# When a late vector is accumulated, and where the softmax reciprocals stand

## The chip, the cores and the metric

The kernel runs on one core of a Trainium2 chip. The metric is device time in microseconds (us) of one execution of the whole program. Shorter is better.

## The reference

A trunk of two layers over a sequence of 1024 tokens of width 1024, all in float32. Layer 0 mixes tokens by forgetting attention with 16 heads, layer 1 by gated linear attention. Each mixer is followed by a SwiGLU channel mixer with 2816 hidden units. Shift, scale and gate of each sub-layer come from six vectors of length 1024 per layer, which are `silu(c)` times a slice of `ada_w`. Cut to what the change touches:

```python
c_act = jax.nn.silu(c)
for i in range(DEPTH):
    mod = c_act @ ada_w[i] + ada_b[i]
    sh1, sc1, g1, sh2, sc2, g2 = jnp.split(mod, N_MOD, axis=-1)
    h = modulate(rms_norm(x, norm1_g[i]), sh1, sc1)
    y = forgetting_attention(h, ...) if i % 2 == 0 else gated_linear_attention(h, ...)
    x = x + g1[:, None, :] * y
    h = modulate(rms_norm(x, norm2_g[i]), sh2, sc2)
    x = x + g2[:, None, :] * swiglu(h, ffn_w_in[i], ffn_w_out[i])

# forgetting attention, per block of 128 queries and head
logits = q @ k.T * scale + cum[q] - cum[k]      # causal
p = jax.nn.softmax(logits, axis=-1)
o = p @ v
```

## The kernel before

**Matrix products** are made of float32 operands split in a high and a low part. Helper `mm3` (L316) issues three matmuls for one product of blocks (L317, L318, L319). The low part of a split is a subtraction on VectorE (`split`, L174: cast on ScalarE at L175, subtraction on VectorE at L176).

**Attention** (L1326 to L1477) works in units (p, a, g): pair of heads p (0 to 7), head a of the pair, and group g of two query blocks of 128 rows. Groups run in the order 0, 3, 1, 2. For each of the two rows of a unit, `scores` (L1327) issues the score matmuls into a ring of two PSUM banks (L1348, L1350, and a mask matmul at L1352), in pieces of up to 512 keys. VectorE adds the forget term to each piece, writes it to the SBUF tile `lp` and takes the row minimum (L1356, a custom instruction and the read of its accumulator into `st`). ScalarE takes the exponential of the whole row and its sum (L1360), VectorE the reciprocal of the sum (L1361), and GpSimd multiplies the row by it (L1362). The next score matmul but one needs the bank that L1356 frees. One unit later, `outputs` (L1365) transposes the finished rows on TensorE (L1382), splits them (L175, L176), multiplies them by the values (L1396, L1394) and adds up the result (L1411, L1412). `weave` (L130) interleaves attention with projections for the next pair of heads (`qk_proj`, whose results go through L894 to L911, and `v_half`), as work that fills TensorE.

**The channel mixer** (`ffn`, L1579) computes its first product in 22 groups (11 blocks of hidden units, gate and up). The first two groups are plain tiles, the other 20 are seven products each of half-size blocks (`prod`, L1733; evacuated by `add`, L1745, and L1905). The weights of each product are loaded to `xv_s`, combined on GpSimd (L978 to L990) and split (L175, L176). The second product runs in three chunks of four groups, of 3, 4 and 4 blocks. The first two chunks are the loop at L1930 (L1956 adds PSUM onto SBUF on VectorE; in the second chunk GpSimd combines blocks at L1970 to L1974 and VectorE applies the gate at L1977). In the second chunk, group by group, GpSimd combines weights (L978 to L980, L996) and then the group's results (L1970 to L1974), while VectorE evacuates, splits weights and applies the gate (L1977) to what GpSimd combined, adding `x` as read back from HBM (loads at L1889). Blocks of hidden units for the third chunk are loaded on SP by `fetch` (L1860); the first block of the third chunk's second tile name, `T1o020`, takes the space of `z2`, which GpSimd reads last at L1973 of the third group, and what follows it in SP's order is issued behind it. The third chunk is at L2024.

**The vectors of layer 1 that are computed beside layer 0's channel mixer:** vectors 5 of layer 0 and 0 of layer 1 go through the queue `ada1` (L543). Vector 1 of layer 1, the scale of its first norm, goes through the queue `ada1l`: `ada_one` (L487) has 16 steps, each a load of 256 KB into `far` (four DMAs at L454 on the SP queue) and two instructions of VectorE that accumulate onto `near` (L497 once, then L499). Each `prod` pays `late_rate[0] * n` into this queue (L1740; n is the depth of the product, 4 in the groups, 3 or 4 in the chunks), and a step is issued when enough has been paid: a load costs 1.5, its two accumulations 0.5. The rate is 0.03 from the start, and 0.12 from the last group but one on (L1902). What is left is flushed behind the second chunk (L1989), and layer 1's first norm needs the vector behind the third.

**Order.** The order in which instructions stand on each engine comes from a list scheduler that works on the whole program. `issue_after`, `behind_one` (L257) and `behind_all` add constraints to it that carry no wait on the chip: an instruction then stands behind another one of the same engine. An engine executes in that order.

## Time and profile before

| | us |
|---|---|
| median of 3 runs | 2345.26 |
| lowest and highest of them | 2344.12, 2349.59 |
| the profiled execution | 2345.56 |
| span of the profiled execution, first to last instruction | 2343.8 |
| attention woven with projections | about 100 to 580 of the span |
| the 20 groups of layer 0's first channel product | about 700 to 1058 |
| first, second and third chunk of its second product | about 1058 to 1130, 1130 to 1205, 1205 to 1250 |

The profile lists for each engine its instructions with start, duration, and, where the engine was idle before one, for how long and which instruction released it. "Idle" and "busy" are of one engine; PE is TensorE, PEld its weight loads, DVE is VectorE, ACT ScalarE, POOL GpSimd, and SP the engine that issues DMAs. Matmuls overlap: 128 partitions by 512 columns take 0.39 us each, and start every 0.23 us. A matmul's end is modelled, so that TensorE reads as busy for a little into every wait.

### The profile page before, as it was taken

What the parts mean: (1) busy time and instruction counts of PE and PEld (TensorE: products, weight loads), DVE (VectorE), ACT (ScalarE), POOL (GpSimd) and SP (SyncE); (2) the same over time, 40 slices, a digit from 0 to 9 for tenths busy, and PEclk for the clock granted to TensorE, in tenths of its full rate; (3) what the DMA queues carried; (4) which work ended last, traced back from release to release, by engine and by line L of the source; (5) the groups of instructions that cost most, each with busy time, mean ns of one, the idle gap of its engine ahead of it and who ended that gap; (6) DMA issues with size and microseconds to landing.
All of it is one profiled execution on the core that took longest, in us unless ns stands there. A gap on an engine that the chain in (4) does not pass through costs nothing.

```text
span 2343.8 us, 35552 instructions
## 1 busy us (share of the span) xinstructions
PE 2322.6 (99%) x12088; PEld 1980.6 (85%) x12088; DVE 1772.7 (76%) x2946; ACT 1128.0 (48%) x2166; POOL 1160.5 (50%) x1027
## 2 busy tenths in 40 slices
PE   8999999999999999999999999999999999999999
PEld 7988888888888888788888899898888888888888
DVE  6577677776788888997888666668787777876787
ACT  6566566675544333334325654345444333345236
POOL 1345454533446656665563522345456666664651
PEclk9999999999999999999999999999999999999999
DMA  8533343352435545459774443555434544458674
GB/s 259 163 99 112 109 120 107 113 169 84 153 100 175 187 158 176 154 203 315 267 265 155 136 128 99 151 171 172 150 102 162 174 147 159 141 189 300 237 264 141
DMA packets 359342, 390.72 MB, mean 167 GB/s; under 512 B 26908, under 2 KB 296376, under 8 KB 359160
## 3 DMA queue, kind: packets, MB, share of 16 engines
q1 hardware_dynamic: 359160, 388.45, 50.7%
q8 instruction: 95, 1.56, 0.3%
q14 instruction: 87, 0.71, 0.1%
HBM read 287.10 MB, written 101.25 MB: 166 GB/s over the span
## 4 chain that ended last, share of the span: by engine, by line
PE 54%; DVE 4%; DMA 3%; POOL 2%; issue 2%; SPq 0%; ACT 0%; POOLq 0%; DVEq 0%; ACTq 0%
PE p_b L317 11%; PE p_b L319 11%; PE p_b L318 11%; PE gv_b L317 1%; PE gv_b L319 1%; PE gv_b L318 1%; PE gr_b L317 1%; PE gr_b L319 1%; PE gr_b L318 1%; DVE o_s L176 1%; DVE ad_s L543 1%; DMA ex_s<-x_sp 1%; PE gqp_b L317 0%; PE gk_b L317 0%; PE f1a_b L319 0%
## 5 line engine op out<-in xcount | busy, mean ns | idle before, releaser
L175 ACT CAST o_s<-xv_s 128x512 fp32r<-128x512 f32 (+1 forms) x392 | 235.9, 610 | 328.4 <-PE p_b L319 218.5
L176 DVE TENSOR_TENSOR o_s<-xv_s,o_s 128x512 fp32r<-128x512 f32 (+1 forms) x392 | 332.7, 854 | 37.2 <-ACT o_s L175 36.3
L317 PE MATMUL p_b<-B,o_s 128*128 128x512 f32 x608 | 235.4, 391 | 0.9 <-DVE ex_s L1745 0.5
L318 PE MATMUL p_b<-B,o_s 128*128 128x512 f32 x608 | 236.1, 389 | 0.0
L319 PE MATMUL p_b<-B,o_s 128*128 128x512 f32 x608 | 235.1, 389 | 0.0
L978 POOL TENSOR_TENSOR ex_s<-xv_s,xv_s 128x512 f32<-128x512 f32 (+1 forms) x64 | 96.0, 1499 | 238.8 <-DMA xv_s<-in_ffn_w_in_dram 123.3
L1362 POOL TENSOR_SCALAR lp_s<-lp_s,st 128x128 f32<-128x128 f32 (+7 forms) x128 | 98.9, 775 | 220.9 <-DVE st L1361 191.8
L317 PE MATMUL p_b<-T,o_s 128*128 128x512 f32 x480 | 186.7, 390 | 1.8 <-DVE x L1745 1.8
L318 PE MATMUL p_b<-T,o_s 128*128 128x512 f32 x480 | 186.7, 389 | 0.0
L319 PE MATMUL p_b<-T,o_s 128*128 128x512 f32 x480 | 181.2, 389 | 0.0
L1360 ACT ACTIVATE lp_s<-lp_s,st 128x128 f32<-128x128 f32 (+7 forms) x128 | 99.5, 777 | 85.4 <-DVE st L1356 68.1
L317 PEld LDWEIGHTS p_b<-B,o_s 128*128 128x128 f32 x608 | 114.1, 188 | 26.6 <-issue 1.6
L319 PEld LDWEIGHTS p_b<-B,o_s 128*128 128x128 f32 x608 | 114.1, 188 | 23.9
L318 PEld LDWEIGHTS p_b<-B,o_s 128*128 128x128 f32 x608 | 114.2, 188 | 23.2
L980 POOL TENSOR_TENSOR xv_s<-ex_s,xv_s 128x512 f32<-128x512 f32 (+1 forms) x64 | 95.7, 1495 | 51.2 <-DVE o_s L176 47.9
L1745 DVE TENSOR_TENSOR ex_s<-ex_s,p_b 128x512 f32<-128x512 f32 x140 | 94.2, 680 | 29.9 <-PE p_b L319 29.6
L990 POOL TENSOR_TENSOR xv_s<-xv_s,xv_s 128x512 f32<-128x512 f32 x48 | 65.8, 1370 | 97.9 <-issue 54.7
L176 DVE TENSOR_TENSOR pt_s<-t_b,pt_s 128x512 fp32r<-128x512 f32 (+1 forms) x160 | 98.4, 632 | 20.3 <-ACT pt_s L175 19.1
L317 PEld LDWEIGHTS p_b<-T,o_s 128*128 128x128 f32 x480 | 90.1, 188 | 21.3 <-DVE x L1745 2.2
L175 ACT CAST pt_s<-t_b 128x512 fp32r<-128x512 f32 (+1 forms) x160 | 82.6, 544 | 51.1 <-PE t_b L1382 32.6
L319 PEld LDWEIGHTS p_b<-T,o_s 128*128 128x128 f32 x480 | 90.1, 188 | 18.7
L318 PEld LDWEIGHTS p_b<-T,o_s 128*128 128x128 f32 x480 | 90.1, 188 | 18.6
(1539 smaller groups left out, 7378.2 us busy)
## 6 DMA issues: line engine op xcount, KB each, us to landing
xv_s<-in_ffn_w_in_dram SPq DMA_DIRECT2D x176, 256.0 KB, 3.2
hid_B<-x SPq DMA_DIRECT2D x66, 512.0 KB, 3.0
ad_s<-in_ada_w_dram SPq DMA_DIRECT2D x384, 64.0 KB, 2.4
hid_T<-x SPq DMA_DIRECT2D x44, 512.0 KB, 2.9
xv_s<-in_ffn_w_out_dram SPq DMA_DIRECT2D x88, 256.0 KB, 3.6
T2o<-hid_T SPq DMA_DIRECT2D x22, 512.0 KB, 7.0
T1o<-hid_T SPq DMA_DIRECT2D x22, 512.0 KB, 6.2
B11o<-hid_B SPq DMA_DIRECT2D x22, 512.0 KB, 5.9
```

Of the source, the lines that this page charges most:

```text
L175: nc.scalar.copy(hi, src)
L176: nc.vector.tensor_sub(lo, src, hi.bitcast(F32))
L317: nc.tensor.matmul(ps, ah, bh, start=start, stop=False, skip_group_check=chain)
L318: nc.tensor.matmul(ps, ah, bl, start=False, stop=False, skip_group_check=chain)
L319: nc.tensor.matmul(ps, al, bh, start=False, stop=stop, skip_group_check=chain)
L543: nc.vector.scalar_tensor_tensor(acc, raw[:, t], c42[:, o:o + 1], acc, op0=ALU.mult, op1=ALU.add)
L978: nc.gpsimd.tensor_add(s1, a21, a22)
L980: nc.gpsimd.tensor_sub(a11, s1, a11)
L990: nc.gpsimd.tensor_sub(r[A12], r[A12], r[A11])
L1360: nc.scalar.activation(lp, lp, AF.Exp, bias=mcur, scale=-1.0, accum_out=st[:, qi, 2:3])
L1362: nc.gpsimd.tensor_scalar(lp, lp, st[:, qi, 3:4], 1.0, op0=ALU.mult, op1=ALU.mult)
L1745: nc.vector.tensor_add(d, d if src is None else dest(G, src), ps)
```

## The change

```diff
--- before.py
+++ after.py
@@ -568,7 +568,7 @@
             while self.q:
                 self(1.0)
 
-    late_rate = [0.03]
+    late_rate = [0.0]
     ada0, ada0p, ada1, ada1l = Pace(), Pace(), Pace(), Pace()
 
     def ada1_queue(js, acc, raws_):
@@ -1358,8 +1358,11 @@
                 mcur = mnew
                 yield max(0.22, 0.00085 * (k1 - k0))
             nc.scalar.activation(lp, lp, AF.Exp, bias=mcur, scale=-1.0, accum_out=st[:, qi, 2:3])
-            nc.vector.reciprocal(st[:, qi, 3:4], st[:, qi, 2:3])
-            nc.gpsimd.tensor_scalar(lp, lp, st[:, qi, 3:4], 1.0, op0=ALU.mult, op1=ALU.mult)
+        at = last_of("D")
+        for qi in range(2):
+            with behind_one("D", at):
+                nc.vector.reciprocal(st[:, qi, 3:4], st[:, qi, 2:3])
+            nc.gpsimd.tensor_scalar(lps[qi], lps[qi], st[:, qi, 3:4], 1.0, op0=ALU.mult, op1=ALU.mult)
         return lps
 
     def outputs(u, lps):
@@ -1899,7 +1902,7 @@
             up = lambda n: advance(n) if X is gs[-1] else None
             if X is gs[-2]:
                 ada1.flush()
-                late_rate[0] = 0.12
+                late_rate[0] = 0.17
                 nxt[0] = part(0)
                 advance(4)
             nc.scalar.copy(dest(X, C11), prod(feed.next(), B11))
```

It has two parts. In `scores` the reciprocal and the multiplication of a row leave the row's loop: they come behind both rows, and each reciprocal is bound to stand behind the unit's last instruction on VectorE (the accumulator read of the last row's last piece). No instruction is added or removed, and no wait. And the late vector is paid for at 0.00 instead of 0.03 in the groups, and at 0.17 instead of 0.12 from the last group but one on. The first load is still issued at the first product, because the queue's account starts at zero.

The scheduler then orders all of attention and layer 0's channel mixer anew; before attention and from the third chunk on, the order of TensorE is the same. Three places are shown. Line numbers in rows of the changed kernel are 3 higher from L1362 on (L1364 is the reciprocal, L1385 the transposition, L1396/L1397 become L1399/L1400 and so on), and numbers at the end of names are those of buffers and tiles.

**VectorE at unit (2, 0, 3)**, the long unit at the start of the third pair of heads. `st203` is its statistics tile and `lp2030`, `lp2031` its two rows; `s206..`, `s207..` are its score pieces. Before:

```order
L1356 ISA lp2030_s45_29_2552,st203_2554<-s206512_b1_52_2562,cum4_s43_5_2034,st203_2554 128x384
L1356 ISA st203_2554 128x1
L176 TENSOR_TENSOR pt1120_s50_38_2500<-t1120_b3_38_2495,pt1120_s50_38_2500 128x512
L1361 RECIPROCAL st203_2554<-st203_2554 128x1
L1356 ISA lp2031_s46_30_2553,st203_2554<-s2070_b0_53_2578,cum4_s43_5_2034 128x512
L1356 ISA st203_2554 128x1
L247 TENSOR_TENSOR w1408_l_s24_24_2691<-w1408__s16_22_2688,w1408_h_s23_23_2690 128x256
L1356 ISA lp2031_s46_30_2553,st203_2554<-s207512_b1_54_2582,cum4_s43_5_2034,st203_2554 128x512
L1356 ISA st203_2554 128x1
L896 SCALAR_TENSOR_TENSOR QA3_2457<-qk031_b7_18_2571,QA3_2457 64x512
L898 SCALAR_TENSOR_TENSOR QB3_2458<-qk031_b7_18_2571,QB3_2458 64x512
L1356 ISA lp201_s47_31_2625,st201_2626<-s2020_b0_55_2627,cum4_s43_5_2034 128x384
```

With the change:

```order
L1356 ISA lp2031_s46_30_2553,st203_2554<-s2070_b0_53_2576,cum4_s43_5_2034 128x512
L1356 ISA st203_2554 128x1
L1356 ISA lp2031_s46_30_2553,st203_2554<-s207512_b1_54_2580,cum4_s43_5_2034,st203_2554 128x512
L1356 ISA st203_2554 128x1
L1364 RECIPROCAL st203_2554<-st203_2554 128x1
L247 TENSOR_TENSOR w1408_l_s24_24_2691<-w1408__s16_22_2688,w1408_h_s23_23_2690 128x256
L896 SCALAR_TENSOR_TENSOR QA3_2457<-qk031_b7_18_2571,QA3_2457 64x512
L898 SCALAR_TENSOR_TENSOR QB3_2458<-qk031_b7_18_2571,QB3_2458 64x512
L176 TENSOR_TENSOR pt2000_s50_41_2610<-t2000_b3_41_2606,pt2000_s50_41_2610 128x384
L1356 ISA lp201_s47_31_2625,st201_2626<-s2020_b0_55_2627,cum4_s43_5_2034 128x384
L1356 ISA st201_2626 128x1
L1364 RECIPROCAL st203_2554<-st203_2554 128x1
```

The first row's reciprocal stood ahead of the second row's first minimum, and now stands behind the second row's last; the second row's follows behind the next unit's first minimum (before, it stood some ten rows further down than shown).

**TensorE at the same place.** `s20..` are score pieces of the pair, `o11..` outputs of the unit before, `t20..` transposed rows, `vps`, `qk` projections that fill. Before, from the second piece of the second row on (its first piece, `s2070`, stands directly ahead):

```order
L1348 MATMUL s207512_b1_54_2582<-KA2_1686,QA2_1684 128x512
L1350 MATMUL s207512_b1_54_2582<-KLA_201,QA2_1684 128x512
L1382 MATMUL t2000_b3_41_2606<-ident_67,lp200_s48_28_2451 128x128 x3
L1348 MATMUL s2020_b0_55_2627<-KA2_1686,QA2_1684 128x384
L1350 MATMUL s2020_b0_55_2627<-KLA_201,QA2_1684 128x384
L1352 LDWEIGHTS identb_72
L1352 MATMUL s2020_b0_55_2627<-maskb_84,identb_72 128x128
L1348 MATMUL s2030_b1_56_2638<-KA2_1686,QA2_1684 128x512
L1350 MATMUL s2030_b1_56_2638<-KLA_201,QA2_1684 128x512
```

With the change, ahead of the next unit's first piece (ahead of the first row shown stand the two matmuls of `s207512` and nine of `o112`):

```order
L317 MATMUL vps20_b6_19_2708<-wv2560_0h_s19_19_2193,h0h2_179 128x256
L1399 MATMUL o112_b5_16_2494<-pt1122_s49_40_2521,v02_s29_3_924 128x256
L1397 MATMUL o112_b5_16_2494<-pt1122_s49_40_2521,v02_s29_3_924 128x128 x2
L318 MATMUL vps20_b6_19_2708<-wv2560_0l_s20_20_2194,h0h2_179 128x256
L319 MATMUL vps20_b6_19_2708<-wv2560_0h_s19_19_2193,h0l2_180 128x256
L317 MATMUL vps20_b6_19_2708<-wv2560_0h_s19_19_2193,h0h3_181 128x256
L318 MATMUL vps20_b6_19_2708<-wv2560_0l_s20_20_2194,h0h3_181 128x256
L1348 MATMUL s2020_b0_55_2627<-KA2_1686,QA2_1684 128x384
L1350 MATMUL s2020_b0_55_2627<-KLA_201,QA2_1684 128x384
```

Five score pieces (`s2070`, `s207512`, `s2020`, `s2030` and, behind the last row shown and its mask, `s2040`) followed each other with no projection between them. Now outputs and five projection matmuls stand between `s207512` and `s2020`.

**VectorE in the groups of layer 0's first product**, where the split weight `o008s` of its ninth block of hidden units is made. `p0_b..` are PSUM banks of products, `o00..`, `o01..` split weights. Before:

```order
L1745 TENSOR_TENSOR ex_s25_7229<-ex_s53_7228,p0_b1_94_9863 128x512
L543 SCALAR_TENSOR_TENSOR ad5_s47_7746<-ad5_s47_7746,c42_165 128x256
L176 TENSOR_TENSOR o008s_s24_108_9900<-ex_s53_7228,o008s_s24_108_9900 128x512
L499 SCALAR_TENSOR_TENSOR near_85<-far_86,c42_165,near_85 128x256 x2
L1745 TENSOR_TENSOR x0_0_6138<-x0_0_6138,p0_b6_91_9804 128x512
L1745 TENSOR_TENSOR ex_s53_7228<-ex_s53_7228,p0_b2_95_9880 128x512
```

With the change:

```order
L543 SCALAR_TENSOR_TENSOR ad5_s47_7746<-ad5_s47_7746,c42_165 128x256 x2
L1748 TENSOR_TENSOR x0_0_6138<-x0_0_6138,p0_b6_91_9774 128x512
L1748 TENSOR_TENSOR ex_s25_7229<-ex_s53_7228,p0_b1_94_9833 128x512
L176 TENSOR_TENSOR o01711_s48_105_9810<-xv_s17_7232,o01711_s48_105_9810 128x512
L176 TENSOR_TENSOR o008s_s24_108_9870<-ex_s53_7228,o008s_s24_108_9870 128x512
L1748 TENSOR_TENSOR ex_s53_7228<-ex_s53_7228,p0_b2_95_9850 128x512
```

The two accumulations of the late vector (L499) are gone from ahead of the evacuation of bank 6 (L1745, with the change L1748), and the evacuation stands ahead of a weight's split. 

**VectorE in the second chunk**, at the start of its second group (`z01`, `x0_2` and `x0_3` are that group's tiles). Before:

```order
L176 TENSOR_TENSOR o031ss_s45_190_11672<-ex_s53_7228,o031ss_s45_190_11672 128x512
L1956 TENSOR_TENSOR z01_10947<-z01_10947,p0_b7_37_11658 128x512
L176 TENSOR_TENSOR o03200_s23_191_11693<-xv_s18_7233,o03200_s23_191_11693 128x512
L1956 TENSOR_TENSOR x0_3_6141<-x0_3_6141,p0_b0_38_11675 128x512
L176 TENSOR_TENSOR o032s_s24_192_11716<-ex_s53_7228,o032s_s24_192_11716 128x512
L1956 TENSOR_TENSOR x0_2_6140<-x0_2_6140,p0_b1_39_11696 128x512
L1956 TENSOR_TENSOR x0_3_6141<-x0_3_6141,p0_b1_39_11696 128x512
L176 TENSOR_TENSOR o03200_s21_193_11735<-xv_s18_7233,o03200_s21_193_11735 128x512
L1956 TENSOR_TENSOR x0_2_6140<-x0_2_6140,p0_b2_40_11721 128x512
```

With the change:

```order
L176 TENSOR_TENSOR o031ss_s45_190_11666<-ex_s53_7228,o031ss_s45_190_11666 128x512
L499 SCALAR_TENSOR_TENSOR near_85<-far_86,c42_165,near_85 128x256
L1959 TENSOR_TENSOR z01_10911<-z01_10911,p0_b7_37_11650 128x512
L499 SCALAR_TENSOR_TENSOR near_85<-far_86,c42_165,near_85 128x256
L176 TENSOR_TENSOR o03200_s23_191_11691<-xv_s18_7233,o03200_s23_191_11691 128x512
L1959 TENSOR_TENSOR x0_3_6141<-x0_3_6141,p0_b0_38_11669 128x512
L176 TENSOR_TENSOR o032s_s24_192_11714<-ex_s53_7228,o032s_s24_192_11714 128x512
L1959 TENSOR_TENSOR x0_2_6140<-x0_2_6140,p0_b1_39_11694 128x512
L1959 TENSOR_TENSOR x0_3_6141<-x0_3_6141,p0_b1_39_11694 128x512
L176 TENSOR_TENSOR o03200_s21_193_11735<-xv_s18_7233,o03200_s21_193_11735 128x512
L499 SCALAR_TENSOR_TENSOR near_85<-far_86,c42_165,near_85 128x256 x2
L1959 TENSOR_TENSOR x0_2_6140<-x0_2_6140,p0_b2_40_11719 128x512
```

Each `L499` is one accumulation. A pair now stands around the second evacuation of `z01`, behind the split `o031ss`, which GpSimd's next combination waits for; the next pair stands behind the group's other evacuations. Seven pairs stand in the second chunk, where none stood: one in the first group ahead of its combinations on GpSimd; then in the second group the two shown and one between the split `o03201` and the gate of `x0_3`; and in the third group three more at the like places. On SP the four DMAs of each of their loads move there too, among the loads of weights (L960), of gate inputs (L1889, with the change L1892) and of blocks (L1860, with the change L1863).

## Prediction

> **What bounds the kernel now.** I read the page's busy times first, then the windows by stage, then the list of waits of TensorE.
>
> ```profile
> span 2343.8 us, 35552 instructions
> ...
> PE 2322.6 (99%) x12088; PEld 1980.6 (85%) x12088; DVE 1772.7 (76%) x2946; ACT 1128.0 (48%) x2166; POOL 1160.5 (50%) x1027
> ```
>
> TensorE is busy for 2322.6 of 2343.8 us, and the change leaves it its work. So all that can be won is in the 21.2 us in which it is idle, in what hides in modelled ends, and in a lowered clock; the rest is whether a new wait opens. The windows give, for each stretch, its length, the busy time of PE, PEld, DVE, ACT and POOL, the granted clock, the DMA share and GB/s:
>
> ```profile
> 232.00:236.00 4.00, 2.39 (x10) 1.14 (x10) 3.86 (x10) 3.27 (x7) 2.63 (x4) 0.97 0.54 155
> 236.00:240.00 4.00, 4.00 (x23) 4.00 (x23) 2.47 (x9) 1.19 (x3) 2.69 (x4) 0.61 0.00 1
> 296.00:300.00 4.00, 2.91 (x21) 2.46 (x20) 3.91 (x11) 1.97 (x5) 1.25 (x2) 1.00 0.34 109
> 100.00:560.00 460.00, 455.04 (x2914) 401.74 (x2913) 332.63 (x881) 290.56 (x615) 224.47 (x321) 1.00 0.39 119
> 700.00:1050.00 350.00, 347.37 (x1529) 285.22 (x1528) 304.13 (x382) 134.44 (x230) 217.01 (x144) 1.00 0.53 173
> 1138.00:1185.00 47.00, 47.00 (x210) 38.89 (x208) 35.98 (x45) 11.00 (x18) 33.30 (x23) 1.00 0.55 176
> 1750.00:2100.00 350.00, 350.00 (x1547) 289.81 (x1546) 270.40 (x340) 136.58 (x233) 220.86 (x148) 1.00 0.48 161
> ```
>
> Attention (100 to 560) loses 4.96 us, the groups of layer 0's first product (700 to 1050) 2.63, and the like groups of layer 1 nothing. The waits of TensorE, with total, number and longest, name the releasers:
>
> ```profile
> PE p_b L317 <- DVE x L1745: 1.8, 1, 1.8
> PE s_b L1348 <- DVE st L1356: 1.5, 2, 1.2
> PE t_b L1382 <- POOL lp_s L1362: 1.0, 1, 1.0
> ...
> PE f0a_b L319 <- DVE o_s L176: 0.8, 1, 0.8
> PE qk_b L317 <- DVE QB L898: 0.7, 1, 0.7
> PE mp_b L460 <- DVE QB L898: 0.6, 1, 0.6
> PE p_b L317 <- DVE ex_s L1745: 0.5, 1, 0.5
> ```
>
> In nearly all of them VectorE stands behind, where it is late for a moment though busy only 76%.
>
> **The change part by part.** The sum is made against the profiled execution, 2345.56 us, which is 0.3 above the median of 2345.26.
>
> *The score run at 232 (−3.3).* The two waits on L1356 lie here: five score pieces follow each other with no projection between them, while VectorE has two instructions for each. The 232 to 236 window lost 1.61 us of busy time and 3% of its clock (0.12), and 236 to 240 ran at 0.61: 0.39 × 4 = 1.56. With the change nine output matmuls and five projections stand between these pieces, so the waits go: 1.61 + 0.12 + 1.56 = 3.3. The clock's part rests on the waits being its cause; the wait at 945, below, speaks against that. *The place at 296 (−1.1).* The window lost 1.09, first a wait on L898, then on L1412; the new order has no such run there. The wait of 0.7 on L898 and that of 1.0 on L1362 lie in an order of TensorE that stays, and I leave them. *New misses (+0.5).* All of attention is ordered anew. Once, in the sixth pair of heads, the new order puts L896 and L898 ahead of a minimum that the score run waits for; between 0 and the 1.2 of the waits above I take 0.5, near the row of L898.
>
> *The moved reciprocals themselves (0).*
>
> ```profile
> L1361 DVE RECIPROCAL st<-st 128x1 f32<-128x1 f32 x128 | 20.3, 160 | 32.8 <-ACT lp_s L1360 31.6
> L1362 POOL TENSOR_SCALAR lp_s<-lp_s,st 128x128 f32<-128x128 f32 (+7 forms) x128 | 98.9, 775 | 220.9 <-DVE st L1361 191.8 <-PE qk_b L318 10.1 <-PE o_b L1394 6.8
> 469.88 1.09 PE L1382 MATMUL t_b<-ident,lp_s 128*128 128x128 f32 x8 [1.00 <-POOL lp_s L1362]
> ```
>
> VectorE sat idle for 31.6 us ahead of reciprocals until the exponential was done. Behind the unit's last minimum the first row's exponential will mostly be done, so idle time of VectorE goes; that is worth nothing by itself, since TensorE does not wait there. In return GpSimd gets the first row later, by up to the second row's minima. GpSimd waits 191.8 us for reciprocals already, and the transposes stand a unit later, so this hides; if it did not, each unit would pay up to the 1.0 us seen once at 469.88.
>
> *The groups (−2.2).*
>
> ```profile
> 944.00:948.00 4.00, 2.24 (x10) 1.57 (x9) 3.96 (x5) 1.30 (x3) 2.22 (x2) 1.00 0.39 120
> 948.00:952.00 4.00, 4.00 (x19) 3.25 (x19) 3.76 (x5) 1.46 (x3) 1.68 (x1) 1.00 0.44 131
> ```
> ```profile
> 945.08 2.02 DVE L499 SCALAR_TENSOR_TENSOR near<-far,c,near 128x256 f32<-128x256 f32 x2
> ...
> 945.61 0.39 PE L318 MATMUL p_b<-T,o_s 128*128 128x512 f32 x1
> ...
> 947.02 0.68 DVE L1745 TENSOR_TENSOR x<-x,p_b 128x512 f32<-128x512 f32 x1
> ...
> 947.75 0.50 PE L317 MATMUL p_b<-T,o_s 128*128 128x512 f32 x1 [1.76 <-DVE x L1745]
> ```
>
> Two accumulations of the late vector keep VectorE for 2.02 us, the evacuation behind them comes late, and TensorE waits 1.76 for its bank; the clock stays at 1.00 in these windows. With the pair gone, and the evacuation ahead, this goes whole. Of the other 0.87 of the 2.63 I take half (the bounds are nothing and, as in layer 1's groups, all): 1.76 + 0.43 = 2.2.
>
> *Ends that hide waits (−0.9).* From 945.61 to 947.75 are 2.14 us from start to start; at the usual pitch of 0.23 the loss is 1.91, not 1.76. So 0.15 of each wait reads as busy; six of the waits go: 0.9.
>
> *The second chunk (+3.3, and +1.7 by the clock).* Its time must be read from a loop between VectorE and GpSimd.
>
> ```profile
> 1143.43 0.75 DVE L1977 SCALAR_TENSOR_TENSOR x<-x,modc,ex_s 128x512 f32<-128x512 f32 x1 [1.56 <-DMA ex_s<-x_sp]
> ...
> 1163.04 0.75 DVE L1977 SCALAR_TENSOR_TENSOR x<-x,modc,ex_s 128x512 f32<-128x512 f32 x1 [1.19 <-POOL x L1970]
> ...
> 1166.17 1.88 DVE L1977 SCALAR_TENSOR_TENSOR x<-x,modc,ex_s 128x512 f32<-128x512 f32 x1 [1.18 <-POOL x L1972]
> ...
> 1206.71 0.70 DVE L1623 TENSOR_TENSOR T3o<-ex_s,T3o 128x512 fp32r<-128x512 f32 x1 [3.22 <-ACT T3o L1622]
> ```
> ```profile
> 1173.13 1.29 POOL L978 TENSOR_TENSOR ex_s<-xv_s,xv_s 128x512 f32<-128x512 f32 x1 [2.73 <-DVE o032ss_s L176]
> ...
> 1185.81 1.29 POOL L1973 TENSOR_TENSOR x<-x,z 128x512 f32<-128x512 f32 x1
> ```
> ```profile
> 1187.13 1.41 SPq L1860 DMA_DIRECT2D T1o<-hid_T  x2
> ```
> ```profile
> SPq L1860 <- POOL x L1973: 2.1, 1, 2.1
> ```
> ```profile
> 1208.80 0.51 PE L319 MATMUL f0a_b<-B11o,o_s 128*128 128x512 f32 x1 [0.82 <-DVE o_s L176]
> ```
>
> VectorE waits for GpSimd ahead of the gates, and GpSimd for VectorE ahead of the next combination; neither waits for TensorE here. From gate to gate the loop takes 1163.04 − 1143.43 = 19.6 us. Its end decides what follows: L1973 at 1185.81 frees the space for T1o, SP issues its load at 1187.13, the T3o blocks are loaded behind it, VectorE waits 3.22 us for their cast, and the split behind it keeps TensorE for 0.82. There is no slack left at that end, so each us by which the loop grows before L1973 is a us of TensorE at 1208. Seven pairs of L499 enter it.
>
> ```profile
> L499 DVE SCALAR_TENSOR_TENSOR near<-far,c,near 128x256 f32<-128x256 f32 x31 | 23.9, 771 | 4.7 <-DMA far<-in_ada_w_dram 4.4
> ...
> L499 DVE SCALAR_TENSOR_TENSOR near<-far,c,near 128x256 f32<-128x256 f32 x13 | 12.8, 985 | 0.1
> ```
> ```profile
> L499 DVE SCALAR_TENSOR_TENSOR near<-far,c,near x31: 469/485/1512, 715.0 to 1125.2; 128x256 f32<-128x256 f32 x31
> ```
>
> The first pair stands where VectorE waits for a DMA anyway (1.56 at 1143.43), and the last behind what L1973 needs: 0 each. Two pairs stand among the evacuations of their groups, ahead of a gate that waits 1.19 for L1970: 0. Two pairs stand behind the split that GpSimd waits for and ahead of the weights' splits, where VectorE has no gap: 4 instructions at 0.47 (the least) to 0.985 (the mean in the groups, beside GpSimd), 1.9 to 3.9. One pair stands ahead of the gate with 1.18 of idle time: 0.9 to 2.0 less 1.18, 0 to 0.8. The sum is 1.9 to 4.7, and I take 3.3. Outer bounds: nothing, or 10 instructions in the loop at 1.51 each, 15.1. TensorE would then wait 0.82 + 3.3 = 4.1 us, more than the waits around 234 that came ahead of the half clock, so I add what that cost: 0.12 + 1.56 = 1.7. The loads of these pairs, 4 issues each on SP, go past the loads of weights and gate inputs; 7 × 256 KB are 39 GB/s over 47 us beside the 176 there, which raises the DMA share from 0.55 to 0.67; I count nothing for them.
>
> **Two rules of the Trainium skill.** On the loop: the window has GpSimd busy for 33.30 of 47 us, and L499 took from 0.469 to 1.512. The Trainium skill ("SBUF — State Buffer", section "Who interferes with whom") says that a VectorE instruction with two inputs from SBUF contends with a GpSimd instruction that reads SBUF, and that the one that comes later waits for all of the other. By it no pair in the loop would be free, 10 × 0.469 = 4.7 in place of 3.3, and the sum 1.4 higher; the two durations agree with it, the gaps of VectorE speak for less. On the clock: the longest wait before the half clock at 236 was 1.21 us. The Trainium skill ("TensorE: Matmul & The Clock Gate", section "HAM oscillation — how this bites in real kernels") gives "no PE-idle gaps >~3.4µs" as the rule. By it the waits at 232 were not the cause, and a gap of 4.1 us would be one; the trace at 945, where 1.76 us left the clock at 1.00, agrees with the first.
>
> **The sum.** −3.3 − 1.1 + 0.5 − 2.2 − 0.9 + 3.3 + 1.7 = −2.0; 2345.6 − 2.0 = 2343.6, and by the median, 0.3 lower, 2343.3 us.
>
> **The rivals.** *The second chunk absorbs the pairs.* If the loop's gaps (1.18 to 1.19 ahead of each gate, 2.73 on GpSimd) take them all, the last two terms go: 2338.3. For it: VectorE is idle for 11.0 of 47 us there, and 14 × 0.771, the mean over the whole trace, are 10.8. Against it: the gaps are where VectorE waits for a GpSimd that it hinders. *Slower: the loop pays each L499 in full.* At 0.985 the ten before L1973 cost 9.9 in place of 3.3, and the sum is +4.6: 2349.8; at 1.51, +9.8: 2355.1. It decides in the loop before 1187, from the point where an instruction costs (5.3 ÷ 10 =) 0.53 us on the mean, since 7.0 are gained before and 1.7 go to the clock. For it: some beside GpSimd took 1.51. Against it: the median was 0.485. *The new order of attention makes as many waits as it removes.* Then 3.3, 1.1 and 0.6 of hidden ends are missing, less the 0.5: −2.0 + 4.5 = +2.5, 2347.8. For it: every order so full of VectorE's work has had such misses, 4.96 us of them here. Against it: the dearest place is visibly filled. *The half clock at 236 stays,* wherever its next wait falls: −2.0 + 1.7 = −0.3, 2345.0.
>
> **How the numbers follow.** Forecast 0.43; absorbed 0.24; slower by the loop 0.14; attention gives nothing 0.10; the clock stays 0.09. A measurement of this kernel can tell about 0.3%, 7.0 us, from no change: faster is below 2338.2, slower above 2352.3. Faster takes half of the absorbed case and a quarter of the forecast (if the clock does not fall at 1208 and the other 2.2 us of attention's 4.96 shrink too): 0.12 + 0.10, with a little of the others 0.23. Slower takes the upper half of the loop's rival and a little of attention's: 0.12. The range: 2335, below the absorbed case by those 2.2 and the other half of the groups, to 2351, between the two prices of the loop's rival.
>
> **What would show it.** Right: no wait of TensorE on L1356 near 232 and a clock of 1.00 at 236 to 240; no wait in 700 to 1050 above 0.5; the gates of the second chunk from 20 to 21 us apart, the load of T1o later against TensorE by about 3, a wait of some 4 us at the third chunk's f0a_b and a lowered clock behind it. Wrong: a wait there of about 0.8 as now (absorbed), of over 8 (the dear loop), or waits of 1 us each at the transposes, one per unit (the moved reciprocals cost after all).

## The result, and the profile after

The changed kernel is slower: 2351.96 us median of 11 runs (2348.19 to 2353.28), against 2347.06 of 11 runs of the kernel before (2344.12 to 2349.59). The ratio is **1.0022, interval 1.0013 to 1.0031**. The profiled execution of the changed kernel took 2349.52 us, 3.96 more than that of before. The forecast was 2343.3, with a range up to 2351: wrong in sign, and just outside the range.

What the change was made of did come. The page, and the windows of the changed kernel (columns as in the prediction):

```profile
span 2347.8 us, 35570 instructions
...
PE 2322.5 (99%) x12088; PEld 1981.5 (84%) x12088; DVE 1771.8 (75%) x2946; ACT 1124.1 (48%) x2166; POOL 1157.4 (49%) x1027
```
```profile
100.00:560.00 460.00, 457.00 (x2946) 404.30 (x2944) 337.74 (x887) 290.42 (x618) 224.38 (x320) 1.00 0.38 119
...
232.00:236.00 4.00, 4.00 (x33) 3.57 (x32) 3.86 (x10) 2.58 (x6) 2.94 (x4) 1.00 0.28 82
236.00:240.00 4.00, 4.00 (x36) 4.00 (x35) 2.52 (x10) 2.31 (x7) 3.71 (x6) 1.00 0.48 184
296.00:300.00 4.00, 4.00 (x35) 3.70 (x34) 2.85 (x13) 2.13 (x8) 3.90 (x6) 1.00 0.50 169
700.00:1050.00 350.00, 350.00 (x1549) 290.00 (x1548) 290.44 (x373) 134.94 (x234) 218.08 (x147) 1.00 0.52 170
1050.00:1250.00 200.00, 189.73 (x811) 153.58 (x810) 161.50 (x213) 68.24 (x127) 106.16 (x74) 0.97 0.79 263
```

The waits at 232 and 296 are gone and the clock stays at 1.00 behind the first; the groups show no idle time any more. The last row is the loss. Before, it read:

```profile
1050.00:1250.00 200.00, 198.99 (x878) 163.59 (x876) 158.89 (x217) 76.28 (x140) 110.17 (x79) 1.00 0.79 268
```

TensorE's idle time in the three chunks grew from 1.01 to 10.27 us, and the clock fell. The waits of TensorE name the places:

```profile
PE f0a_b L317 <- ACT o_s L175: 4.5, 1, 4.5
PE s_b L1348 <- DVE st L1356: 1.7, 3, 1.2
PE p_b L317 <- DMA B22o<-hid_B: 1.7, 2, 1.4
PE f0a_b L319 <- DVE o_s L176: 1.7, 1, 1.7
PE p_b L319 <- DVE o_s L176: 0.9, 2, 0.7
PE p_b L317 <- DVE ex_s L1748: 0.9, 1, 0.9
```

Where the time went is read best from the same matmuls in two traces. Each number below is the start of the first matmul of a product (of the last one in the columns "last") minus that start in the kernel before, from the profiled executions, in us; the split weight's name says which product it is.

| kernel | first product of the channel mixer | first chunk (o020s) | second chunk (o030s) | its second group (o031s) | third chunk, first | third chunk, last | program, last |
|---|---|---|---|---|---|---|---|
| changed | -5.9 | -10.5 | -7.7 | -3.8 | -2.8 | +4.3 | +4.0 |
| e1_attn | -8.3 | -8.2 | -8.2 | -8.2 | -8.2 | -7.2 | -5.5 |
| e2_late | -0.5 | -4.8 | -2.5 | +0.5 | +2.8 | +9.8 | +11.4 |
| e3_none | -5.7 | -9.9 | -9.9 | -9.9 | -10.2 | -11.9 | -12.6 |
| e4_noload | -3.9 | -8.6 | -8.6 | -8.6 | -8.6 | -6.2 | -5.1 |
| e5_noacc | -5.2 | -9.4 | -4.9 | -4.3 | -4.7 | -0.6 | +0.4 |
| e12_issue | -7.6 | -11.7 | -7.2 | -7.2 | -7.5 | -4.9 | -3.3 |
| e6_early | -2.0 | +2.5 | +2.5 | +2.5 | +2.1 | +2.1 | +2.5 |
| e13_012 | -4.2 | -8.8 | -7.1 | -6.0 | -5.0 | +2.2 | +4.1 |
| e14_mid | -6.6 | -11.2 | -8.1 | -4.7 | -4.7 | +2.4 | +2.6 |
| e15_pause | -5.1 | -9.7 | -7.2 | -6.3 | -1.4 | +5.8 | +6.7 |

The changed kernel stood 10.5 us ahead when the first chunk began. It lost 2.8 in that chunk, 3.9 from there to the second group of the second chunk (the seam, below), 1.0 to the end of the second, and 7.1 in the third, nearly all at its start. The first column alone differs by up to 6.3 us between kernels with the same attention (all but e2_late); so differences along a row count, not those between rows.

The start of the third chunk was the forecast's place. VectorE's gates in the second chunk, the load of T1o on SP, and TensorE's waits, of the changed kernel:

```profile
1141.40 0.75 DVE L1980 SCALAR_TENSOR_TENSOR x<-x,modc,ex_s 128x512 f32<-128x512 f32 x1 [1.18 <-POOL x L1973]
...
1162.39 0.75 DVE L1980 SCALAR_TENSOR_TENSOR x<-x,modc,ex_s 128x512 f32<-128x512 f32 x1 [1.18 <-POOL x L1973]
...
1185.51 0.75 DVE L1980 SCALAR_TENSOR_TENSOR x<-x,modc,ex_s 128x512 f32<-128x512 f32 x1 [1.19 <-POOL x L1973]
```
```profile
1190.13 1.76 SPq L1863 DMA_DIRECT2D T1o<-hid_T  x4
```
```profile
1209.13 0.56 PE L317 MATMUL f0a_b<-B11o,o_s 128*128 128x512 f32 x1 [4.49 <-ACT o_s L175]
...
1211.79 0.79 PE L319 MATMUL f0a_b<-B11o,o_s 128*128 128x512 f32 x1 [1.67 <-DVE o_s L176]
```

From the first gate to the third the loop took 44.1 us. Before, the third gate stood at 1182.64, 39.2 behind the first:

```profile
1182.64 0.75 DVE L1977 SCALAR_TENSOR_TENSOR x<-x,modc,ex_s 128x512 f32<-128x512 f32 x1 [1.18 <-POOL x L1970]
```

So the loop grew by 4.9, where 3.3 (1.9 to 4.7) had been forecast. But TensorE began the second chunk 7.7 us earlier than before, and the first gate came only 2.0 earlier (1141.40 against 1143.43): the loop **started 5.7 us later against TensorE**, and that no step had counted. Its start is GpSimd's first combination of the second chunk, which comes 6.2 us later against TensorE (11.7 in place of 5.4 us behind the second chunk's first product of `T1o`). Before, and with the change:

```profile
1133.28 1.56 POOL L978 TENSOR_TENSOR ex_s<-xv_s,xv_s 128x512 f32<-128x512 f32 x1 [9.02 <-DMA xv_s<-in_ffn_w_out_dram]
```
```profile
1131.81 1.72 POOL L978 TENSOR_TENSOR ex_s<-xv_s,xv_s 128x512 f32<-128x512 f32 x1 [12.51 <-DVE near L499]
```

The accumulation that the second row names had itself waited for its load; in e5_noacc, without accumulations, the same instruction waits for its weights, with 13.43 us idle ahead of it. The seam shows what stands ahead of these weights. SP's issues there, before:

```profile
1125.84 0.38 SPq L960 DMA_DIRECT2D xv_s<-in_ffn_w_out_dram  x1
1127.09 0.97 SPq L1860 DMA_DIRECT2D B22o<-hid_B  x2
```

and with the change:

```profile
1122.03 3.56 SPq L454 DMA_DIRECT2D far<-in_ada_w_dram  x4
1125.78 2.75 SPq L960 DMA_DIRECT2D xv_s<-in_ffn_w_out_dram  x2
1129.10 1.92 SPq L1863 DMA_DIRECT2D B22o<-hid_B  x3
```

A load of the late vector occupies SP for 3.56 us directly ahead of weights and of the blocks B22o. In the changed kernel TensorE is 7.7 us early, and B22o goes out 2.0 late. TensorE's wait for it, and the clock behind this wait and behind that of the third chunk:

```profile
1136.04 0.50 PE L317 MATMUL p_b<-B22o,o030ss_s 128*128 128x512 f32 x1 [1.35 <-DMA B22o<-hid_B]
```
```profile
1138.00:1142.00 4.00, 4.00 (x12) 3.07 (x11) 2.83 (x4) 0.95 (x2) 3.37 (x2) 0.60 1.07 381
...
1210.00:1214.00 4.00, 2.33 (x6) 1.82 (x6) 4.00 (x7) 0.62 (x1) 1.11 (x2) 0.50 1.10 353
1214.00:1218.00 4.00, 4.00 (x14) 3.13 (x13) 3.89 (x6) 1.80 (x3) 3.34 (x3) 0.72 1.07 377
```

### The profile page after: what moved, and what is told of

Its sections match the earlier page's. It is cut to its first block, busy times and chain, and to the rows that moved or that the text cites. A ratio compares the mean times of both kernels' runs of the same rounds, so it can differ in the third digit from the quotient of the medians.

```text
span 2347.8 us, 35570 instructions
## 1 busy us (share of the span) xinstructions
PE 2322.5 (99%) x12088; PEld 1981.5 (84%) x12088; DVE 1771.8 (75%) x2946; ACT 1124.1 (48%) x2166; POOL 1157.4 (49%) x1027
## 4 chain that ended last, share of the span: by engine, by line
PE 91%; DMA 5%; DVE 2%; SPq 1%; POOL 1%; issue 1%; ACT 0%; DVEq 0%; POOLq 0%; ACTq 0%
PE p_b L317 15%; PE p_b L319 15%; PE p_b L318 15%; PE o_b L1399 3%; PE t_b L1385 2%; PE qk_b L317 2%; PE qk_b L319 2%; PE qk_b L318 2%; PE s_b L1348 1%; PE s_b L1350 1%; PE vps_b L317 1%; PE vps_b L318 1%; PE vps_b L319 1%; PE gv_b L317 1%; PE gv_b L319 1%; PE gv_b L318 1%
## 5 line engine op out<-in xcount | busy, mean ns | idle before, releaser
L978 POOL TENSOR_TENSOR ex_s<-xv_s,xv_s 128x512 f32<-128x512 f32 (+1 forms) x64 | 96.3, 1504 | 245.9 <-DMA xv_s<-in_ffn_w_in_dram 118.6
L980 POOL TENSOR_TENSOR xv_s<-ex_s,xv_s 128x512 f32<-128x512 f32 (+1 forms) x64 | 93.1, 1455 | 58.7 <-DVE o_s L176 55.9
L1748 DVE TENSOR_TENSOR ex_s<-ex_s,p_b 128x512 f32<-128x512 f32 x140 | 94.4, 682 | 35.9 <-PE p_b L319 35.8
L247 POOL TENSOR_TENSOR w_l_s<-w__s,w_h_s 128x256 fp32r<-128x256 f32 x90 | 70.1, 807 | 80.9 <-ACT w_h_s L243 80.1
L318 PEld LDWEIGHTS p_b<-T,o_s 128*128 128x128 f32 x480 | 90.1, 188 | 18.6
L319 PEld LDWEIGHTS p_b<-T,o_s 128*128 128x128 f32 x480 | 90.1, 188 | 18.6
```

Source lines behind the costliest of these rows:

```text
L247: (nc.gpsimd if i < 3 else nc.vector).tensor_sub(lo[:, cs], rw[:, cs], hi[:, cs].bitcast(F32))
L318: nc.tensor.matmul(ps, ah, bl, start=False, stop=False, skip_group_check=chain)
L319: nc.tensor.matmul(ps, al, bh, start=False, stop=stop, skip_group_check=chain)
L978: nc.gpsimd.tensor_add(s1, a21, a22)
L980: nc.gpsimd.tensor_sub(a11, s1, a11)
L1748: nc.vector.tensor_add(d, d if src is None else dest(G, src), ps)
```

## The experiments

The theory after the result: the gains are real and would be kept; the late vector's move costs more than both, in the chunks. The first rival: the chunks are held by their transfers anyway, so that whatever is gained ahead of them is waited for there. All ratios are to the kernel before; an interval is some 0.001 to each side, 2.3 us, so that a difference of two ratios is uncertain by 3 to 4 us. The scheduler orders other instructions of the chunks anew in most of these kernels, on SP too, so no pair of them differs in one thing alone; e2_late has the order of the changed kernel there.

### The two parts apart, and no late vector

The part in attention alone (`e1_attn`):

```diff
-    late_rate = [0.0]
+    late_rate = [0.03]
...
-                late_rate[0] = 0.17
+                late_rate[0] = 0.12
```

> The part in attention alone; the late vector is paid for as before (0.03, then 0.12). Theory (what attention gains is kept, and the late vector alone costs in the chunks): TensorE comes out of attention about 6 us earlier, as in the changed kernel, and keeps it to the end: ratio to before about 0.9974 (0.9965 to 0.9985). Rival (the chunks are held by their transfers, so that whatever is gained ahead of them is waited for there): the 6 us are gone by the third chunk, ratio 0.999 to 1.001, with new waits of TensorE between 1050 and 1140.

Measured: **0.998** (0.9972 to 0.9989). `e2_late` has the rates 0.0 and 0.17 in the kernel before, with its attention:

> The part on the late vector alone (0.00, then 0.17); attention as before. Theory: the groups gain about 4.3 us, the first chunk and its end lose about 6.8, the second chunk and the start of the third some 8: net +10, ratio 1.0035 to 1.005. Rival (the chunks are held by their transfers): TensorE arrives 6 us later than in the changed kernel, so less is waited for, net about +4, ratio 1.001 to 1.003.

Measured: **1.0043** (1.0029 to 1.0056). `e3_none` leaves all steps but the first of the late vector out of the changed kernel:

```diff
-        for n in range(16):
+        for n in range(1):
...
-            if n < 15:
+            if n < 0:
                 ada_load(raw, l, j, n + 1, 2)
```

> The changed kernel without steps 2 to 16 of the late vector (neither their loads nor their accumulations; the vector is left out but for its first step). Theory: no loss in the chunks, and the 10.5 us gained ahead of them are kept, and the wait of 0.8 at the third chunk is no larger: ratio 0.9945 to 0.9965. Rival: the chunks still wait for their transfers, ratio 0.998 to 1.000.

Measured: **0.9944** (0.9932 to 0.9957). All three came as the theory had it, e3_none at the edge of its range. 0.998 and 1.0043 add up to the 1.0022 of both. In e1_attn TensorE carries its lead from 635 us to the third chunk without a loss (table, -8.3 to -8.2), though the first chunk holds six loads of the late vector, as before. And e2_late, which reaches the first chunk 5.7 us later than the changed kernel, loses 2.3 there and 3.0 at the seam, where the changed kernel loses 2.8 and 3.9: TensorE's early arrival is not what costs. The chunks' own transfers do not hold TensorE; e3_none in the same stretch:

```profile
1050.00:1250.00 200.00, 199.77 (x882) 165.09 (x881) 155.15 (x204) 76.89 (x139) 108.13 (x77) 1.00 0.72 249
```

With the late vector 1.0022, without it 0.9944: 0.0078, or 18.3 us, is what it costs where the change puts it.

### Loads or accumulations

`e4_noload` keeps the accumulations of the changed kernel, but only the first load; `e5_noacc` keeps the loads, but only the first two accumulations:

```diff
             if n < 15:
-                ada_load(raw, l, j, n + 1, 2)
                 yield 1.5
```

> The changed kernel with all accumulations of the late vector but only the first of its loads (steps 2 to 16 accumulate the first step's block again, so the vector is wrong but for its first step). Theory A (the accumulations lengthen the loop of VectorE and GpSimd in the second chunk, the loads cost only in the first chunk): the first chunk loses nothing, the gates of the second chunk stay 21 to 23 us apart and TensorE waits 3 to 6 us at the third chunk: ratio 0.998 to 1.000. Theory B (the loads, which wait on SP for the one buffer, are the cause of all): the gates are 19.6 to 20.3 us apart, the wait at the third chunk is below 1.5: ratio 0.9945 to 0.997.

```diff
-                for t in range(2):
+                for t in range(2 if n == 0 else 0):
```

> The changed kernel with all loads of the late vector but only its first two accumulations (the vector is left out but for its first step). The loads then wait only for each other, not for VectorE. The loads cost 12.7 us in the pair of runs without them and without both (0.9968 to 1.0022) as long as the accumulations are there. Theory Q (what costs is that a load waits on SP for the accumulation that still reads the one buffer, and weights and blocks stand behind it): nearly nothing of it is left, ratio 0.9945 to 0.9965. Rival D (their bytes cost, where the DMA engines are full): the 12.7 us stay but for the accumulations' own 5.6, ratio 0.9985 to 1.001.

Measured: **0.9968** (0.9957 to 0.998) and **0.9990** (0.9981 to 0.9999). The first ratio lies in theory B's range, but the signs are mixed: the first chunk loses nothing (theory A), the gates are 21.9 us apart (A) and then 19.6 (B). The second lies in rival D's range. Above 0.9944, the accumulations alone cost 0.0024, 5.6 us, and the loads alone 0.0046, 10.8 us. The accumulations cost nothing at the seam (table, -8.6 throughout) and then at the third chunk's start, where the forecast had its terms of 3.3 + 1.7:

```profile
PE f0a_b L317 <- ACT o_s L175: 2.3, 2, 1.5
...
PE f0a_b L319 <- DVE o_s L176: 0.9, 1, 0.9
```

The loads take the larger share, which the prediction had priced at nothing. Neither number is what the part costs in the changed kernel, because each part alone comes earlier: the accumulations of e4_noload end 31 us behind the second chunk's first product of `T1o`, in place of 69, and the loads of e5_noacc 36 us behind it, in place of 63. Theory Q, that a load costs because it waits on SP for the accumulation that still reads its buffer, foretold 0.9945 to 0.9965 for e5_noacc and falls in that form: without accumulations the loads still cost. They also wait for each other, as SP's waits of e5_noacc show:

```profile
SPq L454 <- DMA far<-in_ada_w_dram: 6.6, 2, 4.4
```

What each does to the second chunk's loop can be read in the traces, from its first gate to that of its third group:

| accumulations in the loop | kernels | length of the loop, us |
|---|---|---|
| none, and no loads | before, e1_attn, e3_none, e6_early | 39.2 each |
| none, with loads | e5_noacc, e12_issue | 37.7, 38.4 |
| 4 | e4_noload, e14_mid | 41.5, 41.1 |
| 8 | e13_012 | 43.2 |
| 10 | changed, e2_late, e9_small | 44.1, 43.8, 43.0 |
| 12 | e15_pause | 45.8 |

So accumulations lengthen the loop, by 0.4 to 0.6 us each, and loads do not. (It is longer still, 46.0 with 10 and 55.9 with 12, in e8_act and e10_one, below, which load the vector in other ways.) What the loads do is to make the loop late: its first gate stands 13.6 us behind the second chunk's first product of `T1o` without either (e3_none), 15.0 with accumulations alone (e4_noload), and 19.6 with loads alone (e5_noacc), where the first L978 waits for its weights.

### Bytes, or the time on the queue

`e9_small` cuts the loads from the second on to 32 of 256 columns, with the accumulations as they are; `e12_issue` does so without the accumulations. Both leave most of the vector out.

```diff
-                ada_load(raw, l, j, n + 1, 2)
+                ada_load(raw, l, j, n + 1, 2, 32)
```

> The changed kernel with the loads of steps 2 to 16 of the late vector cut to 32 of 256 columns (an eighth of the bytes, the same number of DMAs and the same waits; most of the vector is left out). Theory Q (the queue on SP): as the changed kernel, ratio 1.000 to 1.0025. Rival D (bytes): as without the loads, ratio 0.9965 to 0.998.

> The changed kernel with all DMAs of the late vector at an eighth of their bytes and without its accumulations from the second step on (the vector is left out but for its first step). What is left of the late vector on the path is the issuing on SP and each load's wait for the one before. With the full bytes this gave 0.9990, without loads 0.9944. Theory I: 0.997 to 0.999, most of the 10.8 us stays. Rival D (bytes): 0.9945 to 0.9965.

Measured: **1.0002** (0.9993 to 1.0011) and **0.9977** (0.9968 to 0.9987), as theory Q had the first and theory I the second. At an eighth of the bytes and without accumulations, the loads still cost 0.0033 above 0.9944, 7.7 us. The full bytes add 0.0013 (3.1 us, no more than the uncertainty) without accumulations and 0.0020 (4.7 us) with them. So most of the loads' cost does not need their bytes. What is left of them is the time that their 60 issues, and the waits of these, take on SP ahead of other transfers; that this is the cost is argued, since the order of other transfers changes with it. In SP's waits from 1040 to 1215, the kernel before has the first of these rows and the changed kernel the second:

```profile
SPq L454 <- DVE near L499: 1.9, 2, 1.4
```
```profile
SPq L454 <- DVE near L499: 12.2, 5, 3.1
```

I then tried to take the issues away. `e10_one` makes one DMA of each four in the changed kernel, `e11_attn_one` does the same in e1_attn; `e8_act` lets ScalarE issue them:

```diff
+            nc.sync.dma_start(raw, src.rearrange("(r t) (q c) -> q r t c", t=nt, q=4))
```

> The changed kernel with one DMA per step of the late vector in place of four, from its second step on; the same bytes, accumulations and waits. Theory I (28 issues of 0.57 us each, 16 us of SP, stand in the second chunk ahead of weights and blocks, and as many in the first): three quarters of that go, ratio 0.998 to 1.0005. Theory W (what costs is that SP waits for the buffer, not the issuing): ratio 1.001 to 1.0025 as the changed kernel.

> The part in attention as changed, the late vector paid for as before (0.03, then 0.12), but with one DMA per step in place of four. Against the part in attention alone (0.998): theory I: the first chunk, which holds nine of its steps, gains a little, ratio 0.9965 to 0.998. Theory W: 0.9975 to 0.9985.

```diff
-                ada_load(raw, l, j, n + 1, 2)
+                ada_load(raw, l, j, n + 1, 2, nc.scalar)
```

> The changed kernel with the loads of steps 2 to 16 of the late vector issued by ScalarE instead of SP; the computation is whole. Theory Q (the queue on SP): weights and blocks no longer stand behind them, and ScalarE, half idle here, takes the waits: ratio 0.997 to 1.000, the wait at the third chunk below 4 us. Rival D (bytes): ratio 1.001 to 1.003 as now. If ScalarE's own queue holds up its casts, it comes out above 1.003.

Measured: **1.0134** (1.012 to 1.0148), **1.0058** (1.0044 to 1.0072) and **1.0057** (1.0045 to 1.007). Neither theory holds for the first two; e8_act took the last of its cases. None of the three tells issuing from waiting. From the issue of one DMA of 256 KB to the accumulation behind it e10_one takes 8.4 us (median of 15), where the changed kernel takes 6.3 from the first of four issues, and its VectorE waits for every load:

```profile
DVE near L504 <- DMA far<-in_ada_w_dram: 53.5, 15, 7.8
```

In the changed kernel this wait was 9.9 us in all (7 times), in the kernel before 4.4. On ScalarE the loads hold up other work; TensorE's waits of e8_act name a copy of ScalarE:

```profile
PE p_b L317 <- ACT x L1957: 3.8, 1, 3.8
```

### The place of the loads

`e6_early` pays 0.06 throughout, so that the vector ends in the groups; `e13_012` pays nothing in the groups and 0.12 behind, `e14_mid` 0.02 and 0.12.

> The part in attention as changed, and the late vector paid for at 0.06 throughout, so that it ends in the groups, ahead of both chunks. Theory (the chunks are where it costs): the chunks lose nothing (-1 to -3 against before), the groups lose about twice their 4.3 us, attention keeps its 6: ratio 0.9965 to 0.999. Rival (VectorE is too full in the groups, 87% with half of these instructions): the groups lose 10 us or more, ratio 0.9995 to 1.002.

> The changed kernel with a rate of 0.12 in place of 0.17 from the last group but one on (nothing in the groups, as changed). The late vector is whole; its last steps come at the end of the second chunk. Theory P (the first chunk loses because the faster pace puts loads into SP's order where the buffer is not yet free, and before it held six of them at 0.12 for nothing): the first chunk loses under 1.5 us, the third chunk's start 8 as now or more, ratio 0.999 to 1.001. Rival (any load in the first chunk costs once TensorE arrives 10 us earlier): it loses 4 to 7 as now, ratio 1.0015 to 1.003.

> As changed in attention; the late vector at 0.02 in the groups and 0.12 behind, so that about five steps stand in the groups and three in the second chunk. Theory P: the groups lose 2 to 3 us, the first chunk under 1.5, the third chunk's start 2 to 4: ratio 0.997 to 0.999, about as the attention part alone (0.998). Rival: 0.999 to 1.001, because the first chunk loses as in the changed kernel.

Measured: **0.9982** (0.9973 to 0.9991), **1.0003** (0.9994 to 1.0012) and **1.0003** (0.9994 to 1.0012). e6_early bears the place out from the other side: its chunks are as before, and the price moves into the groups, both read in its windows and in its row of the table (from -2.0 to +2.5 in the groups, and +2.1 to +2.5 behind). Its profiled execution, 2348.06, is the longest of its runs; their median is 2343.32.

```profile
1050.00:1250.00 200.00, 199.29 (x881) 164.69 (x881) 153.49 (x199) 77.15 (x140) 112.99 (x80) 1.00 0.75 259
...
700.00:1050.00 350.00, 344.98 (x1511) 281.45 (x1510) 312.37 (x393) 131.07 (x225) 216.42 (x143) 1.00 0.54 175
```

e13_012 lost 2.8 instead of 6.7 us up to the second group of the second chunk; theory P had under 1.5 there, though its ratio came. e14_mid, with three loads left for the second chunk and the old pace, lost 6.5 there, and its ratio is the rival's; so the faster pace is not needed for the loss. What goes with the loss is the time of four SP and VectorE events against the second chunk's first product of T1o, from the traces, in us:

| kernel | last load ahead of B22o | first issue of B22o | first gate | issue of T1o | length of the third chunk |
|---|---|---|---|---|---|
| before | -12.4 | -0.8 | 15.6 | 59.3 | 56.3 |
| e1_attn | -12.5 | 0.3 | 17.0 | 60.7 | 57.3 |
| e3_none | none | -3.8 | 13.6 | 57.3 | 54.7 |
| e4_noload | none | -3.1 | 15.0 | 61.0 | 58.7 |
| e5_noacc | -8.4 | 4.0 | 19.6 | 61.8 | 60.4 |
| e13_012 | -4.1 | 5.6 | 19.4 | 67.1 | 63.5 |
| e14_mid | 1.9 | 8.4 | 22.7 | 68.3 | 63.4 |
| changed | 1.9 | 8.9 | 21.2 | 70.0 | 63.4 |

In the main, the closer the last load stands to the seam, the later B22o and the first gate. The issue of T1o follows from the first gate and the length of the loop, and the end of the third chunk goes with it: that chunk's last matmul starts 69.9 to 73.0 us behind the issue of T1o in all sixteen kernels, though T1o itself goes out anywhere from 57.3 to 83.4 behind that product. So a us by which the loop ends later is about a us of TensorE, as the forecast had it. Against before, T1o goes out 10.7 later in the changed kernel: 5.7 by the late start and 4.9 by the longer loop. TensorE uses B22o at 13.6 to 14.2 in all of them. `e15_pause` moves the loads off the seam and keeps their number:

```diff
+                if (c_, i) in ((0, 2), (1, 1)):
+                    late_rate[0] = 0.25 * c_
```

> The changed kernel with nothing paid for the late vector from the third group of the first chunk to the first of the second, and 0.25 from there (0.17 before the pause), so that no load of it stands on SP close ahead of the blocks B22o and the gate inputs of the second chunk; the vector is whole. Theory S (what costs is a load that waits on SP at the seam of the chunks; B22o goes out 9 to 11 us behind the second chunk's first product in the changed kernel, -1 to 3 before, and is used at 13.6): B22o goes out at 5 or earlier, no wait on it, the second chunk's first gate at 15 to 18 us in place of 21.2, the load of T1o at 63 to 66 in place of 70, the third chunk's stretch 60 to 62 us in place of 63.4: ratio 0.9985 to 1.0005. Rival (the number of loads and accumulations, wherever they stand): ratio 1.0015 to 1.003 as the changed kernel.

Measured: **1.0018** (1.0009 to 1.0027), in the rival's range. Theory S came in half of its signs only: the last load stands at -9.1, B22o goes out at 3.4, TensorE's waits on it shrink from 1.7 to 0.4 us, and the seam costs 0.9 in place of 3.9 us (table of positions, -7.2 to -6.3). But the first gate is at 20.0, where the theory had 15 to 18, and the accumulations that were taken off the seam now lengthen the loop: 45.8 in place of 44.1. T1o goes out at 73.2, and the rest of the second chunk costs 4.9 in place of 1.0. The loss at the seam goes with a load that stands there; moving that load elsewhere in the second chunk wins nothing.

## Why the prediction was wrong, step by step

- **The score run and the place at 296 (-4.4), new misses (+0.5), the moved reciprocals (0).** Right in sign and in place. The part alone gave 0.998, 4.7 us, against 4.4 − 0.5 and 0.6 of hidden ends; the lead of 5.9 us at 635 us is of one trace, and such leads differ by some us between traces. The new miss stands in the sixth pair, where the order had shown it, and cost 10.00 − 8.43 = 1.57 idle instead of 0.5 (before, this window had no idle time). No wait on the transposes came.

```profile
408.00:418.00 10.00, 8.43 (x60) 7.47 (x59) 7.72 (x19) 7.50 (x16) 6.59 (x10) 1.00 0.30 92
```

- **The groups (-2.2).** Right, and too small: all 2.63 of idle time went, and the lead grew by 4.6 from the first product to the first chunk. The other 2.0 show in no idle time; ends that hide waits, of which I had counted 0.15 each for six, are a guess for them.
- **The second chunk's loop (+3.3), the half clock (+1.7).** The mechanism was right and the sizes were low. The loop grew by 4.9 for ten accumulations, 0.49 each on the mean, where I had counted four as free. The clock ran at 0.50 and 0.72 in two windows of 4 us behind the third chunk's wait, 2.0 + 1.1 = 3.1 lost; at the seam it ran at 0.60, another 1.6, behind a wait of 1.35 that the forecast had not seen. The wait at the third chunk, 4.49 and then 1.67, is near the 4.1 forecast by luck: T1o goes out 10.7 later against TensorE, in place of 3.3, but TensorE itself loses 4.9 between the second chunk's first product of T1o and the third chunk.
- **The loads: "I count nothing for them."** This is the step that failed. I had asked whether the DMA engines have room and not what stands behind a load on SP's queue. (The share of 0.55 was a mean over 47 us; in 1130 to 1146 it was 1.06 already before.) The loads alone cost 10.8 us, of them 7.7 without most of their bytes. In the changed kernel, what the forecast has no term for is 2.8 in the first chunk, 3.9 at the seam, and a loop that starts 5.7 later against TensorE; these overlap in time and are no sum. The first chunk holds six loads as before, but a seventh now stands at the seam.
- **The rivals.** The loop that pays each L499 in full named the right place and 2349.8, 2.2 us below the measured median, by luck: its price was 0.985 each, and the loop grew by 0.49 each; the loads, which it had at nothing too, made up the difference. The rule of the Trainium skill ("SBUF — State Buffer", section "Who interferes with whom") that a later instruction waits for the whole of the other gave 4.7 for ten accumulations; it came nearer to the loop's 4.9 than my 3.3. The loop did not absorb the pairs, and the half clock at 236 did not stay.

Still open: in the 7.7 us of loads with few bytes, how much is issuing, how much waiting for the one buffer, and how much the new order of other transfers. A second buffer, which would tell the first two apart, was not tried.

Of the versions run, e1_attn (0.998) and e6_early (0.9982) beat both kernels and are whole; the intervals do not tell them apart.

## What to carry to other kernels

Work that is moved takes its transfers along, and they can cost more than the work. Before moving it, look at what stands behind each of them on the issuing queue, how long it waits there for its buffer, and how many us ahead of its use the transfer behind it is issued: here 13 us ahead brought no wait (e1_attn), 8 to 10 one of 0.3 to 0.4 us (e13_012, e5_noacc, e15_pause), and 5 waits of 1.7. A lead that is gained earlier need not shorten that distance: in e1_attn TensorE came 8.2 us earlier, and B22o went out only 1.1 later against it.

## What was not expected of the hardware

With one DMA of 256 KB in place of four of 64 KB, VectorE waited 53.5 us for 15 loads, where it waited 9.9 in the changed kernel, and the kernel took 1.34% more than before (the changed one 0.22%). And the same wait at the sixth pair (8.43 busy of 10 us in both) left the clock at 1.00 in the changed kernel, above, but at 0.86 in e13_012:

```profile
408.00:418.00 10.00, 8.43 (x52) 7.49 (x50) 7.62 (x21) 7.29 (x15) 6.58 (x10) 0.86 0.31 92
```

So whether a wait of this size lowers the clock is not settled by its length; the forecast's term for it stays a chance.
